# A decoder layer's gate rows by DMA, a put-off weight remainder and two exchanged PSUM pools

## The chip, the cores and the metric

The kernel runs on one core of one Trainium2 chip. The metric is device time in microseconds (us) of one execution, taken as the median of several runs.

## The reference

One inference step of a two-layer decoder: 256 prompt tokens and 64 sample tokens (8 sequences of 8) share the weights. Layer 0 mixes tokens with a gated MLP, layer 1 with an mLSTM, and each is followed by a gated MLP with a short convolution. The change lies in the mLSTM, of 8 heads with keys of 128 and values of 256. What matters of it, cut:

```
m_t = max(inter, max(D))             # D = b_t - b_s + i_s, inter = b + m
w_intra = exp(D - m_t);  w_inter = exp(inter - m_t)
sc  = (q k^T) * w_intra
num = w_inter * (q C) + sc v
den = w_inter * (q n) + sum(sc)
h   = num / max(|den|, exp(-m_t))
C_new = decay * C + (k * g)^T v      # decay = exp(bL + m - m_new)
hn  = (h - mean(h)) * rsqrt(var(h) + eps) * gain
y   = (sigmoid(o) * hn) @ w_out
```

The prompt starts from an empty state; each of the 8 sample sequences has a state C of its own, which is read and written back.

## The kernel before

**Layout.** Activations lie with features on the partitions and the 320 tokens along the free dimension. Each fp32 weight block of 128 columns (a tile `raw`, 512 KB) comes by DMA on SP's queue and is split into two parts, `wh` by a cast on ScalarE and the remainder `wl = raw - wh` by VectorE (`prefetch`, lines 120 to 157). A product is three matmuls per 128 rows: wh with xh, wh with xl, wl with xh. In this layer `low_last` is set, so that a block issues its 16 matmuls with wh first and the 8 with wl last (`chunk`, line 173). There are four buffers of `raw` and three each of `wh` and `wl`; taking a block starts the load of the fourth block behind it and the split of the next one (`take`, line 165).

**PSUM.** There are two pools of banks: `psm` with three, mostly for the blocks (`pm`), and `psa` with five, for everything else. A tile takes the bank that came free first, so that in psm the tile after next but one waits for the readers of the present one, in psa the fifth after it.

**Order.** TensorE's order is the program's, pinned by `mm` and `tr`. The other engines' order comes from a planner that runs instructions by program order among those that it holds ready, by its own costs; `tc.issue_after(x)` sets instructions behind x on x's engine, and `pin` keeps one in the program's order. Each engine, and each DMA queue, then works strictly in its order.

**Gates (line 661).** From the gate weights the kernel makes, for all heads at once, rows of eight partitions, `Xf`, 392 long: 320 running maxima, 64 factors for the sample tokens and 8 decays of the states. They are kept in two parts in `X`. `sel` (128 x 8 x 128) holds for each head a matrix that picks its row and spreads it over all partitions.

**Heads (lines 1057 to 1115).** Iteration h goes through six blocks: q (`qk_epi(h, 0)`), k, two of v (`v_epi`), two of the output gate (`o_epi`, line 993). Between them lies the end of head h-1: its states' part (`inter`), `numer`, `stats`, `state_prompt`, and its four pairs of state updates, `state_sample(h-1, 0..3)`, each with two matmuls into `pcs` (one bank in psa, one in psm up to head 5), two updates of `C` on VectorE and a store. `scores(h)` (line 789) spreads the head's row over the partitions with a matmul into `pMb` (`sel[:, h]` against `X`), makes the scores `psc`, the weights `w` from pMb by three Exp on ScalarE with masks by GpSimd, copies the decays to `dec`, and scales the sample's queries to `qw`. Behind the second gate block come `finish(h-1)` (transposes of `hn` into two tiles `phn`, then `y_b`, `yhb`, `ylb`, line 1000), `state_sample(h-1, 3)`, `k_nat(h)` (three transposes into `pk`, line 855), `v_nat(h)` (six into two tiles `pv`) and `inter(h, 0)` (into `num`). For h = 4, 5 and 6 blocks of the output projection (`early`) are put in.

**stats (line 931)** makes mean, variance and denominator of `num`; GpSimd raises to the power -1/2 (`sl`, line 953), VectorE makes the bias `nb` (line 957), and ScalarE writes the normalised `hn`. In the last head a function `between`, with the first gate block's end and a split of weights, stands ahead of `nb`.

**Tail (lines 1118 to 1149).** For the last head two banks of psm hold begun output blocks (`begin`), so that the two gate blocks share the third.

The lines that say most:

```
1101                if h and not last:
1102                    o_epi(h, 1, blk())
1103                if h and not last:
1104                    finish(h - 1)
1105                    state_sample(h - 1, 3)
1106                k_nat(h)
1107                v_nat(h)
```

Of the kernel before, what the change touches and what calls it, by code (L numbers as in the profile page):

```python
# [37 lines left out]
class Net:  # L38
# [26 lines left out]
    def weights(self):  # L65

        I = self.I
        q = []

        def add(w, b, *groups, k0=0):  # L70
            for kn in groups:
                q.append((w, b, k0, kn))
                k0 += kn


        add(I["a_wv"], 0, 4)
        add(I["a_wv"], 4, 4)
        add(I["a_wv"], 0, 4, k0=4)
        for b in range(1, 4):
            add(I["a_wv"], b, 4, 4)  # L80
        add(I["a_wv"], 4, 4, k0=4)
        for b in range(5, 16):
            add(I["a_wv"], b, 8)
        for b in range(16):
            add(I["a_win"], b, 8)
        for b in range(KD):
            add(I["a_wo"], b, 8, 8)

        def ffn(l):
            for b in range(2 * KF):  # L90
                add(I["f_up"][l], b, 8)
            for b in range(KD):
                add(I["f_dn"][l], b, 8, 7, 7)

        ffn(0)
        add(I["b_wg"], 0, 8)
        for h in range(NH):
            for r in range(6):
                r = (0, 2, 1, 3, 4, 5)[r] if h == 0 else r
                if (h, r) == (NH - 1, 4):  # L100
                    for k0, n in ((8, 4), (12, 2)):
                        for b in (0, 1):
                            add(I["b_wo"], b, n, k0=k0)
                add(I["b_win"], 6 * h + r, 8)
                for b in self.EARLY_OUT.get((h, r), ()):
                    add(I["b_wo"], b, 8)
        add(I["b_wo"], 2, 6, k0=8)
        for b in (0, 1, 2):
            add(I["b_wo"], b, 2, k0=14)
        for b in range(3, KD):  # L110
            add(I["b_wo"], b, 8, k0=8)
        ffn(1)
        self.wq = q
        self.loaded, self.halved, self.used = [], [], 0

    AHEAD, SPLIT_AHEAD = 4, 1
    low_last = False
# [2 lines left out]
    def prefetch(self, n, m):  # L120

        nc = self.nc
        while len(self.loaded) < min(n, len(self.wq)):
            w, b, k0, kn = self.wq[len(self.loaded)]
            raw = self.wraw.tile([P, 8, P], F32, tag="raw", name="raw")
            for j, z in ((0, 2), (2, 4)) if len(self.loaded) < 2 else ((0, kn),):
                self.hold(nc.sync.dma_start(raw[:, j:z, :], w[b, :, k0 + j:k0 + z, :]))
            self.loaded.append(raw)
        while len(self.halved) < min(m, len(self.wq)):
            i = len(self.halved)  # L130
            raw, kn = self.loaded[i], self.wq[i][3]
            self.loaded[i] = None
            wh = self.wsp.tile([P, 8, P], F32R, tag="wh", name="wh")
            wl = self.wsp.tile([P, 8, P], F32R, tag="wl", name="wl")
            if self.wq[i][0] is self.I["b_wg"]:

                nc.scalar.copy(wh[:, :, 64:], raw[:, :, 64:])
                nc.scalar.copy(wl[:, :, :64], raw[:, :, :64])
                nc.vector.tensor_tensor(wl[:, :, 64:], raw[:, :, 64:], wh[:, :, 64:].bitcast(F32), op=SUB)
                self.halved.append((None, wl))  # L140
                continue
            if i < 2:

                a, z = slice(0, 2), slice(2, 4)
                if not i:
                    self.hold(nc.vector.tensor_copy(wh[:, a, :], raw[:, a, :]))
                    self.x_parts(0)
                for c in (a, z)[not i:]:
                    self.last_split = self.hold(nc.scalar.copy(wh[:, c, :], raw[:, c, :]))
                for c in (a, z):  # L150
                    self.last_low = self.hold(nc.vector.tensor_tensor(wl[:, c, :], raw[:, c, :], wh[:, c, :].bitcast(F32), op=SUB))
                self.halved.append((wh, wl))
                continue
            self.last_split = self.hold(nc.scalar.copy(wh[:, :kn, :], raw[:, :kn, :]))  # L154
            self.last_low = nc.vector.tensor_tensor(wl[:, :kn, :], raw[:, :kn, :], wh[:, :kn, :].bitcast(F32), op=SUB)  # L155
            self.hold(self.last_low)
            self.halved.append((wh, wl))

    @contextmanager
    def behind_split(self):  # L160
# [21 lines left out]
                if sweep:  # L182
                    self.mm(ps[:, :T], wl[:, k, :], xh, False, last and k == kn - 1)

    def block(self, kt, rhs):

        ps = self.psm.tile([P, 512], F32, tag="pm", name="pm")
        done = 0
        while done < kt:
            kn = self.wq[self.used][3]  # L190
            self.chunk(ps, lambda k: rhs(done + k), done == 0, done + kn == kt)
            done += kn
        return ps
# [441 lines left out]
    def layer_b(self):  # L635
# [5 lines left out]
        with ExitStack() as ctx:  # L641
# [3 lines left out]
            gnh = lp.tile([P, 16], F32, name="gnh")  # L645
            colsT = lp.tile([P, 3, 96], F32, name="cols")
            X = lp.tile([P, 392], F32R, name="X")
            sel = lp.tile([P, NH, P], F32R, name="sel")
            mk = lp.tile([P, NB], F32, name="mk")
            mo = lp.tile([8, 9], F32, name="mo")  # L650
            pads = []
# [9 lines left out]
            def gates(rp):  # L661

                bif = rp.tile([40, 1 + NB], F32, name="bif")
                rst = rp.tile([40, 2, T], F32, name="rst")
                selr = rp.tile([P, NH, P], F32, name="selr")
                RS = rp.tile([P, 384], F32, name="RS")
                nc.sync.dma_start(bif, I["b_if"])
                nc.sync.dma_start(rst, I["seg"])
# [54 lines left out]
                nc.vector.tensor_tensor(seg(wi[:, :64]), m0.unsqueeze(2).to_broadcast([8, NB, NS]), seg(M[:, TP:]), op=SUB)  # L723
                nc.vector.tensor_tensor(wi[:, 64:72], m0, ML, op=SUB)
                nc.scalar.activation(Xf[:, T:392], wi, AF.Exp)
                nc.vector.tensor_copy(X[0:8], Xf)
                nc.vector.tensor_tensor(X[32:40], Xf, X[0:8].bitcast(F32), op=SUB)
                nc.vector.tensor_scalar(gnh, self.vecs[:, V_GN:V_GN + 16], 0.5, None, op0=MULT)
# [54 lines left out]
            def v_epi(h, j, ps):  # L783
# [2 lines left out]
                nc.scalar.copy(vT[:, T:384], ps[:, TP:T])  # L786
                S[h].setdefault("vT", []).append(vT)

            def scores(h):
                s = S[h]  # L790
                q, qh, ql = s["q"]
                k, kh, kl = s["k"]
                pb = self.psa.tile([P, 512], F32, tag="pa", name="pMb")
                sc = self.psa.tile([P, 512], F32, tag="pa", name="psc")
                if h:
                    mm(pb[:, :392], sel[:, h, :], X, True, True)
                mm3(sc[:, :TP], kh, kl, qh, ql, True, True)
                mm(sc[:, TP:384], k[:, P:TP], q[:, P:TP], True, True)
                mm(sc[:, 384:448], k[:, TP:384], q[:, TP:T], True, True)
                if not h:  # L800

                    mm(pb[:, :392], sel[:, h, :], X, True, True)
                w = hp.tile([P, 448], F32, tag="w", name="w", bufs=1)
                for (n, o, c0, c1, t) in ((P, 0, 0, TP, 0), (P, TP, P, TP, 1), (64, 384, TP, T, 2)):
                    nc.scalar.activation(w[:n, o:o + c1 - c0], pb[:n, c0:c1], AF.Exp, scale=-1.0, bias=colsT[:n, t, h:h + 1])
                for o in (0, TP):
# [4 lines left out]
                                        channel_multiplier=1)  # L811
                nc.gpsimd.affine_select(w3, w3, pattern=[[NS, NB], [1, NS]], compare_op=ALU.is_ge, fill=0.0, base=0,
                                        channel_multiplier=-1)
                dec = hp.tile([P, NB], F32, tag="dec", name="dec", bufs=2)
                nc.vector.tensor_copy(dec, pb[:, 384:392])
                qw = hp.tile([P, 64], F32, tag="qw", name="qw", bufs=1)
                nc.vector.scalar_tensor_tensor(qw, q[:, TP:T], 0.5, pb[:, T:384], op0=MULT, op1=MULT)
                Qd = Qz.rearrange("p (b e) -> p b e", e=136)
# [36 lines left out]
            def k_nat(h):  # L855
                s = S[h]
                ks = s["k"][0]
                pk = self.psa.tile([P, 512], F32, tag="pa", name="pk")
                for t in range(3):
                    self.tr(pk[:, t * P:(t + 1) * P], ks[:, t * P:(t + 1) * P], self.ident)  # L860
                kgh = hp.tile([P, 2, P], F32R, tag="kgh", name="kgh", bufs=1)
# [69 lines left out]
            def stats(h, between=None):  # L931
# [17 lines left out]
                t1 = hp.tile([P, 3], F32, tag="t1", name="t1", bufs=1)  # L949
                nc.vector.scalar_tensor_tensor(t1, rd, EPS, rd, op0=MULT, op1=MULT)  # L950
                self.t_made = nc.vector.scalar_tensor_tensor(t1, t1, 1e-36, mv[:, :, 1], op0=MAX, op1=ADD)
                sl = hp.tile([P, 3], F32, tag="sl", name="sl", bufs=1)
                nc.gpsimd.tensor_tensor(sl, t1, self.mhalf.to_broadcast([P, 3]), op=ALU.pow)
                if between:
                    between()
                nb = hp.tile([P, 3], F32, tag="nb", name="nb", bufs=1)
                made = nc.vector.scalar_tensor_tensor(nb, mv[:, :, 0], -1.0, sl, op0=MULT, op1=MULT)
                if between:
                    self.pin(made)
                for t in range(3):  # L960
                    n = P if t < 2 else 64
                    if h == NH - 1 and t:
# [37 lines left out]
            def finish(h):  # L1000
# [3 lines left out]
                for e in range(2):  # L1004
# [1 line left out]
                    for t in range(3):  # L1006
                        self.tr(pt[:, t * P:(t + 1) * P], hn[:, t, e * P:(e + 1) * P], self.ident)
                    y = self.tp.tile([P, T], F32, tag="yf", name="y_b", bufs=2)
                    nc.vector.scalar_tensor_tensor(y, s["o"][e], 1.0, pt[:, :T], op0=ADD, op1=MULT)
                    g = gnh[:, 2 * h + e:2 * h + e + 1]  # L1010
                    nc.scalar.activation(yh[:, e, :], y, AF.Copy, scale=g)
                    nc.vector.scalar_tensor_tensor(yl[:, e, :], y, g, yh[:, e, :].bitcast(F32), op0=MULT, op1=SUB)
# [43 lines left out]

            for h in range(NH):
                if h:
                    qk_epi(h, 0, blk())
                    early(h, 0)  # L1060
                    if h == 1:
# [35 lines left out]
                if h:  # L1097
                    state_in(h)
                    for i in (0, 1):
                        state_split(h, i)  # L1100
                if h and not last:
                    o_epi(h, 1, blk())
                if h and not last:
                    finish(h - 1)
                    state_sample(h - 1, 3)
                k_nat(h)
# [26 lines left out]
            v_first(h)  # L1133
            state_prompt(h)
            k_mask(h)
            o_epi(h, 1, blk())
            finish(h)
            state_sample(h, 0)
            begin(2)
            state_sample(h, 1)  # L1140
            for m in range(KD):
                ps = part.get(m)
# [61 lines left out]
def _lay_out(i):  # L1204
# [55 lines left out]
    seg[:, 0, starts] = 0.0  # L1260
    seg[:, 1, starts] = -1e30
    a["seg"] = seg
    sel = np.zeros((P, NH, P), f)
    for h in range(NH):
        sel[h, h] = 1.0
        sel[32 + h, h] = 1.0
    a["sel"] = sel

    b, q = np.arange(NB), s // 32
# [30 lines left out]
```

## Time and profile before

| | |
|---|---|
| median of 3 runs | 956.14 us (955.89 to 956.53) |
| the profiled execution's own time | 956.05 us |
| its span, first to last instruction | 954.3 us |
| TensorE / VectorE / ScalarE / GpSimd busy | 99% / 73% / 56% / 12% |
| mean granted TensorE clock | 0.999 |
| mean DMA rate | 163 GB/s |

The span is what the trace covers; about 1.7 us of the execution lie outside it. A row of a timeline has the start in us from the span's start, the length in us, engine, line, operation, what is written and from what, and a count; in square brackets stands how long the engine sat idle just before, and which instruction ended that. Matmuls overlap, so their cost is the distance between starts and not their length.

### The profile page before, as it was taken

How to read it: one execution, taken by the hardware profiler on the slowest of the kernel's cores; microseconds unless marked ns; L12 is line 12 of the kernel's file. 1: busy time of each engine (PE TensorE's matmuls, PEld its weight loads, DVE VectorE, ACT ScalarE, POOL GpSimd, SP SyncE). 2: the span in 40 equal slices, each digit the busy share in tenths (PEclk: the TensorE clock that was granted, in tenths of full speed). 3: DMA queues.
4: the chain of work that ended last, by engine and by line, in shares of the span. 5: the costliest groups of instructions: out<-in, count | busy, mean ns of one | idle time of the engine just before them, and what ended most of it. 6: DMA issues, size and time to landing. Idle time of an engine off the chain costs nothing.

```text
span 954.3 us, 17131 instructions
## 1 busy us (share of the span) xinstructions
PE 947.3 (99%) x6427; PEld 933.8 (98%) x6427; DVE 697.3 (73%) x1331; ACT 531.9 (56%) x978; POOL 115.8 (12%) x291
## 2 busy tenths in 40 slices
PE   9999999999999999999999999999999999999997
PEld 8889999999999999999999999999999999999997
DVE  6766976577777754559999998788897777775443
ACT  7557543454555443458777876666766445544342
POOL 2200000010000000014333322102102000000000
PEclk9999999999999999999999999999999999999999
DMA  8643346444444465565465655553474444445441
GB/s 270 210 153 133 133 137 198 160 146 147 149 156 155 139 183 147 149 216 175 128 212 175 206 178 196 185 183 118 132 247 148 149 145 154 156 144 155 143 141 56
DMA packets 54214, 155.19 MB, mean 163 GB/s; under 512 B 7372, under 2 KB 11980, under 8 KB 54132
## 3 DMA queue, kind: packets, MB, share of 16 engines
q1 hardware_dynamic: 54132, 154.10, 50.5%
q8 instruction: 51, 0.84, 0.4%
q14 instruction: 31, 0.25, 0.1%
HBM read 142.10 MB, written 11.97 MB: 161 GB/s over the span
## 4 chain that ended last, share of the span: by engine, by line
PE 94%; DVE 3%; ACT 1%; POOL 1%; DMA 0%; issue 0%; SPq 0%; POOLq 0%
PE pm L54 81%; PE pv_a L54 6%; PE num L54 2%; PE pmix L54 1%; PE pcs L54 1%; PE psc L54 1%; PE phn L57 0%; PE pCp L54 0%; DMA raw<-in_a_wv 0%; PE pv L57 0%; DVE wl L155 0%; PE pc L54 0%; DVE bcv L767 0%; PE pg L54 0%; PE pk L57 0%
## 5 line engine op out<-in xcount | busy, mean ns | idle before, releaser
L154 ACT CAST wh<-raw 128x1024 fp32r<-128x1024 f32 (+3 forms) x256 | 257.0, 1004 | 294.1 <-PE pm L54 161.7
L155 DVE TENSOR_TENSOR wl<-raw,wh 128x1024 fp32r<-128x1024 f32 (+3 forms) x256 | 299.0, 1169 | 118.9 <-ACT wh L154 115.0
L54 PE MATMUL pm<-xh,wh 128*128 128x320 f32 x1216 | 372.3, 311 | 0.1
L54 PE MATMUL pm<-xl,wh 128*128 128x320 f32 x1216 | 370.3, 309 | 0.0
L54 PE MATMUL pm<-xh,wl 128*128 128x320 f32 x1216 | 321.2, 309 | 0.0
L54 PEld LDWEIGHTS pm<-xh,wh 128*128 128x128 f32 x1216 | 228.4, 188 | 0.4 <-DVE o_b L995 0.3
L54 PEld LDWEIGHTS pm<-xl,wh 128*128 128x128 f32 x1216 | 228.4, 188 | 0.2
L54 PEld LDWEIGHTS pm<-xh,wl 128*128 128x128 f32 x1216 | 214.5, 188 | 0.0
L54 PE MATMUL pm<-yh_f,wh 128*128 128x320 f32 x352 | 108.8, 309 | 0.0
L54 PE MATMUL pm<-yl_f,wh 128*128 128x320 f32 x352 | 108.8, 309 | 0.0
L54 PE MATMUL pm<-yh_f,wl 128*128 128x320 f32 x352 | 108.8, 309 | 0.0
L54 PEld LDWEIGHTS pm<-yh_f,wh 128*128 128x128 f32 x352 | 66.1, 188 | 0.0
L54 PEld LDWEIGHTS pm<-yl_f,wh 128*128 128x128 f32 x352 | 66.1, 188 | 0.0
L54 PEld LDWEIGHTS pm<-yh_f,wl 128*128 128x128 f32 x352 | 66.1, 188 | 0.0
L531 DVE SCALAR_TENSOR_TENSOR fcv<-fpad,vecs,fcv 128x336 f32<-128x336 f32 x88 | 49.6, 565 | 2.1 <-ACT fcv L529 0.7
L54 PE MATMUL pm<-yh_a,wh 128*128 128x320 f32 x128 | 39.6, 310 | 0.0
L54 PE MATMUL pm<-yh_a,wl 128*128 128x320 f32 x128 | 39.5, 309 | 0.0
L54 PE MATMUL pm<-yl_a,wh 128*128 128x320 f32 x128 | 39.5, 309 | 0.0
L533 ACT ACTIVATE fgl<-fcv 128x256 f32<-128x256 f32 x44 | 18.2, 414 | 37.8 <-DVE fcv L531 37.8
L54 PE MATMUL pm<-yhb,wh 128*128 128x320 f32 x128 | 38.1, 311 | 0.0
L54 PE MATMUL pm<-ylb,wh 128*128 128x320 f32 x128 | 37.8, 309 | 0.0
L303 DVE TENSOR_TENSOR xT<-pm,xT 128x320 f32<-128x320 f32 x39 | 19.1, 489 | 25.1 <-PE pm L54 24.9
(286 smaller groups left out, 1371.7 us busy)
## 6 DMA issues: line engine op xcount, KB each, us to landing
raw<-in_f_up SPq DMA_DIRECT2D x88, 512.0 KB, 3.3
raw<-in_b_win SPq DMA_DIRECT2D x48, 512.0 KB, 4.0
raw<-in_f_dn SPq DMA_DIRECT2D x32, 448.0 KB, 3.3
C<-in_C SPq DMA_DIRECT2D x32, 258.0 KB, 3.7
out_Cs<-C SPq DMA_DIRECT2D x32, 258.0 KB, 2.5
raw<-in_a_win SPq DMA_DIRECT2D x16, 512.0 KB, 3.3
raw<-in_a_wo SPq DMA_DIRECT2D x16, 512.0 KB, 4.3
raw<-in_f_dn SPq DMA_DIRECT2D x16, 512.0 KB, 3.5
```

The lines of the kernel that those rows point to most:

```text
L54: self.pin(self.nc.tensor.matmul(out, lhsT, rhs, start=start, stop=stop, skip_group_check=skip))
L154: self.last_split = self.hold(nc.scalar.copy(wh[:, :kn, :], raw[:, :kn, :]))
L155: self.last_low = nc.vector.tensor_tensor(wl[:, :kn, :], raw[:, :kn, :], wh[:, :kn, :].bitcast(F32), op=SUB)
L303: self.nc.vector.tensor_tensor(x, ps[:, :T], x, op=ADD)
L531: nc.vector.scalar_tensor_tensor(cv, pd[:, i:i + NC], self.vec(w + i * KF), cv, op0=MULT, op1=ADD)
L533: nc.scalar.activation(gl[:, :TP], cv[:, :TP], AF.Gelu_apprx_tanh)
```

## The change

It has seven edits, all but the small `sel` in or for the heads' loop:

- `Xf` is stored to a DRAM tensor `rows`, and each head from 1 on loads its row from there into all partitions, a tile `Mb` of two buffers. Head 0 keeps the matmul. `sel` shrinks to head 0's matrix.
- For these heads `dec` is a part of `Mb`, and isn't copied.
- In heads 1 to 6 the remainder `wl` of the block behind the second gate block is put off until the first `y_b` of `finish`.
- `pk` takes its bank in psm, but for the last head.
- `nb` is made by GpSimd from the negated mean, ahead of `between`.
- The last head's second gate block takes its bank in psa.
- Behind `begin(2)` one more block is split ahead.

The small name for it is "with two such transposes": `finish` transposes into two tiles as before; nothing in the diff touches that.

```diff
@@ prefetch
             self.last_split = self.hold(nc.scalar.copy(wh[:, :kn, :], raw[:, :kn, :]))
-            self.last_low = nc.vector.tensor_tensor(wl[:, :kn, :], raw[:, :kn, :], wh[:, :kn, :].bitcast(F32), op=SUB)
-            self.hold(self.last_low)
             self.halved.append((wh, wl))
+            self.late.append((wl[:, :kn, :], raw[:, :kn, :], wh[:, :kn, :]))
+            if not self.put_off:
+                self.low_parts()
+
+    def low_parts(self):
+
+        for wl, raw, wh in self.late:
+            self.last_low = self.hold(self.nc.vector.tensor_tensor(wl, raw, wh.bitcast(F32), op=SUB))
+        self.late = []
@@ gates
-            sel = lp.tile([P, NH, P], F32R, name="sel")
+            sel = lp.tile([P, P], F32R, name="sel")
...
                 nc.scalar.activation(Xf[:, T:392], wi, AF.Exp)
+
+                nc.sync.dma_start(I["rows"], Xf)
@@ scores
+            def rows_in(h):
+                mb = hp.tile([P, 392], F32, tag="Mb", name="Mb", bufs=2)
+                nc.sync.dma_start(mb, I["rows"][h:h + 1, :].to_broadcast([P, 392]))
+                S[h]["rows"] = mb
...
-                pb = self.psa.tile([P, 512], F32, tag="pa", name="pMb")
+                pb = s["rows"] if h else self.psa.tile([P, 512], F32, tag="pa", name="pMb")
...
-                if h:
-                    mm(pb[:, :392], sel[:, h, :], X, True, True)
...
-                    mm(pb[:, :392], sel[:, h, :], X, True, True)
+                    mm(pb[:, :392], sel, X, True, True)
...
-                dec = hp.tile([P, NB], F32, tag="dec", name="dec", bufs=2)
-                nc.vector.tensor_copy(dec, pb[:, 384:392])
+                dec = pb[:, 384:392]
+                if not h:
+                    dec = hp.tile([P, NB], F32, name="dec")
+                    nc.vector.tensor_copy(dec, pb[:, 384:392])
@@ k_nat
-                pk = self.psa.tile([P, 512], F32, tag="pa", name="pk")
+                pool, tag = (self.psm, "pm") if h < NH - 1 else (self.psa, "pa")
+                pk = pool.tile([P, 512], F32, tag=tag, name="pk")
@@ stats
+                nm = hp.tile([P, 3], F32, tag="nm", name="nm", bufs=1)
+                nc.vector.tensor_scalar(nm, mv[:, :, 0], -1.0, None, op0=MULT)
                 sl = hp.tile([P, 3], F32, tag="sl", name="sl", bufs=1)
                 nc.gpsimd.tensor_tensor(sl, t1, self.mhalf.to_broadcast([P, 3]), op=ALU.pow)
+                nb = hp.tile([P, 3], F32, tag="nb", name="nb", bufs=1)
+                nc.gpsimd.tensor_tensor(nb, nm, sl, op=MULT)
                 if between:
                     between()
-                nb = hp.tile([P, 3], F32, tag="nb", name="nb", bufs=1)
-                made = nc.vector.scalar_tensor_tensor(nb, mv[:, :, 0], -1.0, sl, op0=MULT, op1=MULT)
-                if between:
-                    self.pin(made)
@@ finish
-                    nc.vector.scalar_tensor_tensor(y, s["o"][e], 1.0, pt[:, :T], op0=ADD, op1=MULT)
+                    made = nc.vector.scalar_tensor_tensor(y, s["o"][e], 1.0, pt[:, :T], op0=ADD, op1=MULT)
+                    if self.put_off:
+                        self.put_off = False
+                        with tc.issue_after(made.ins):
+                            self.low_parts()
@@ the heads' loop
                 if h:
+                    rows_in(h)
                     qk_epi(h, 0, blk())
...
                 if h and not last:
+                    self.put_off = True
                     o_epi(h, 1, blk())
-                if h and not last:
                     finish(h - 1)
                     state_sample(h - 1, 3)
@@ the tail
-            o_epi(h, 1, blk())
+            o_epi(h, 1, self.block(KD, self.x_rhs, self.psa.tile([P, 512], F32, tag="pa", name="pm")))
             finish(h)
             state_sample(h, 0)
             begin(2)
+            self.prefetch(0, self.used + 2)
```

`block` gets an argument for a PSUM tile of the caller's.

More of the change, by code (lines that the diff above doesn't have):

```diff
@@ L114, in weights @@
         self.loaded, self.halved, self.used = [], [], 0
+        self.late, self.put_off = [], False
     AHEAD, SPLIT_AHEAD = 4, 1
@@ L183, in chunk, with block @@
                     self.mm(ps[:, :T], wl[:, k, :], xh, False, last and k == kn - 1)
-    def block(self, kt, rhs):
-        ps = self.psm.tile([P, 512], F32, tag="pm", name="pm")
+    def block(self, kt, rhs, ps=None):
+        if ps is None:
+            ps = self.psm.tile([P, 512], F32, tag="pm", name="pm")
         done = 0
@@ L664, in gates @@
                 rst = rp.tile([40, 2, T], F32, name="rst")
-                selr = rp.tile([P, NH, P], F32, name="selr")
+                selr = rp.tile([P, P], F32, name="selr")
                 RS = rp.tile([P, 384], F32, name="RS")
@@ L1262, in _lay_out @@
     a["seg"] = seg
[L1263 to L1266, printed above, removed]
+    sel = np.zeros((P, P), f)
+    sel[[0, 32]] = 1.0
     a["sel"] = sel
@@ L1282 @@
     I = {k: nc.dram_tensor("in_" + k, v.shape, F32, kind="ExternalInput").ap() for k, v in arrays.items()}
+    I["rows"] = nc.dram_tensor("rows", (NH, 392), F32).ap()
     O = {k: nc.dram_tensor("out_" + k, s, F32, kind="ExternalOutput").ap() for k, s in _OUTS.items()}
```

## The prediction

> **What bounds the kernel now.** I read the page first, for the busy shares.
>
> ```profile
> span 954.3 us, 17131 instructions
> PE 947.3 (99%) x6427; PEld 933.8 (98%) x6427; DVE 697.3 (73%) x1331; ACT 531.9 (56%) x978; POOL 115.8 (12%) x291
> ```
>
> TensorE (PE) is busy for 99% of the span. So time can be won in two ways only: fewer matmuls, or fewer of PE's waits. All edits but the small selector lie in the mLSTM layer's loop over heads, about 446 to 694 us. Next I read the view of stretches there: one between heads 1 and 2, one head of six weight blocks, one of eight.
>
> ```profile
> 479.70:489.30 9.60, 9.60 (x71) 9.60 (x70) 9.42 (x20) 8.34 (x17) 4.37 (x6) 1.00 0.62 195
> 508.20:536.70 28.50, 28.50 (x209) 28.49 (x209) 26.82 (x66) 21.91 (x51) 10.00 (x13) 1.00 0.59 181
> 565.20:604.35 39.15, 39.15 (x282) 39.14 (x281) 32.19 (x72) 25.17 (x54) 6.91 (x13) 1.00 0.57 184
> ```
>
> After the length come PE, weight loads, VectorE (DVE), ScalarE and GpSimd (POOL) busy, then the clock, 1.00. DVE is second: 98% behind head 1, 94% in head 3, 82% in head 5. Third, the waits of PE's weight loads in the whole layer, of which two can be touched:
>
> ```profile
> PEld pv L57 <- DVE y_b L1009: 0.8, 1, 0.8
> PEld pm L54 <- DVE o_b L995: 0.3, 1, 0.3
> ```
>
> **The selector matmul.** Seven of the eight pMb matmuls go (heads 1 to 7). What one costs is the distance of two starts on PE's timeline, since matmuls overlap.
>
> ```profile
> 525.91 0.34 PE L54 MATMUL pMb<-X,sel 128*128 128x392 f32 x1
> 526.10 0.28 PE L54 MATMUL psc<-qh,kh 128*128 128x256 f32 x1
> ```
>
> 526.10 − 525.91 = 0.19 us, by times rounded to 0.01; I take 0.18. PE never waits there, so all of it is on the path: 7 × 0.18 = **1.26 us** less. The Trainium skill, "TensorE: Matmul & The Clock Gate", section "Wait — 56ns, not 53.3ns?", gives columns ÷ 2.4 GHz plus about 2.5 ns for a warm start-to-start: an estimate of 166 ns for 392 columns, and of 1.16 us for seven. The trace's 0.19 us is longer, and the sum keeps the trace.
>
> **Its replacement** is one 12.5 KB store and seven loads of 128 × 1568 B = 196 KB on SP's queue. Nearest rows:
>
> ```profile
> C<-in_C SPq DMA_DIRECT2D x32, 258.0 KB, 3.7
> gB<-in_a_ln_g SPq DMA_DIRECT2D x4, 128.0 KB, 5.0
> ```
>
> The second is also a row repeated over partitions. So a load lands 3.7 to 5.0 us after issue; I take 5.0. It is issued at a head's start and wanted in its scores, four blocks of 3.5 us later: 14 us of cover. I cost it at 0. Each load waits on SP for the reader of the buffer two heads back, the last state update, and weight loads queue behind it; the store of that same update waits there now, so the place of the wait isn't new. The small selector shortens one cast on ScalarE in head 0's gates, of which PE waits for nothing; and ScalarE and DVE read the row from SBUF instead of PSUM, off PE's path. Both 0.
>
> **Head 1's wait.** PE's timeline in head 1, and the same two steps in head 5:
>
> ```profile
> 476.93 0.49 PE L57 MATMUL pk<-ident,qs 128*128 128x128 f32 x3
> 477.26 0.60 PE L57 MATMUL pv<-ident,vTb 128*128 128x128 f32 x4
> 478.44 0.44 PE L57 MATMUL pv<-ident,vTb 128*128 128x128 f32 x2 [0.58 <-DVE y_b L1009]
> 478.93 0.36 PE L54 MATMUL num<-Ch,Qz 128*128 128x258 f32 x1
> ...
> 603.04 0.82 PE L57 MATMUL pv<-ident,vTb 128*128 128x128 f32 x6
> 603.62 0.36 PE L54 MATMUL num<-Ch,Qz 128*128 128x258 f32 x1
> ```
>
> From pv to num head 5 takes 0.58 us, head 1 takes 1.67: the wait costs 1.09. The second pv tile is the fifth psa bank after the first phn, so it waits for the y_b that reads phn. DVE at that time:
>
> ```profile
> 473.45 1.21 DVE L155 TENSOR_TENSOR wl<-raw,wh 128x1024 fp32r<-128x1024 f32 x1
> 474.58 0.55 DVE L311 TENSOR_TENSOR Pl<-Pf,Ph 128x384 fp32r<-128x384 f32 x1
> ...
> 476.37 1.22 DVE L155 TENSOR_TENSOR wl<-raw,wh 128x1024 fp32r<-128x1024 f32 x1
> ...
> 477.91 0.87 DVE L1009 SCALAR_TENSOR_TENSOR y_b<-th_o,phn 128x320 f32<-128x320 f32 x2
> ```
>
> ```profile
> 473.31 0.51 ACT L311 CAST Ph<-Pf 128x384 fp32r<-128x384 f32 x1 [0.30 <-DVE Pf L824]
> ```
>
> There are 256 such wl, as many as weight chunks, so counting in queue order tells whose each is: the one at 473.45 is head 2's first block, which the change puts behind the first y_b; the one at 476.37 belongs to the block after and stays. Without the former, DVE moves up until Pl meets its input at 473.82: by 0.7 us. The first y_b then ends near 478.39 − 0.7 = 477.7. With pk in psm, one bank fewer is asked of psa, so the next to wait is num, which PE reaches at 478.93 − 1.09 − 0.18 = 477.66. About 0.1 is left: **1.0 us** gained. The bounds are 0 (DVE only carries the lateness on) and 1.09.
>
> **What putting off costs.** In head 3:
>
> ```profile
> 527.95 1.22 DVE L155 TENSOR_TENSOR wl<-raw,wh 128x1024 fp32r<-128x1024 f32 x1
> ...
> 534.45 0.49 DVE L995 TENSOR_TENSOR o_b<-pm,rb 128x320 f32<-128x320 f32 x1 [0.53 <-PE pm L54]
> 534.86 0.88 DVE L1009 SCALAR_TENSOR_TENSOR y_b<-th_o,phn 128x320 f32<-128x320 f32 x2
> ```
>
> ```profile
> 538.88 1.34 PE L54 MATMUL pm<-xh,wl 128*128 128x320 f32 x8
> ```
>
> The wl of 527.95 would run behind the first y_b, from about 535.3 to 536.5, and PE reads it at 538.88: 2.4 us to spare. The raw buffer comes free some 7 us later, inside a lead of four blocks. Queued behind it on DVE are the second y_b, state updates, k and v remainders, all about 1.13 us later (start to start, 473.45 to 474.58). The tightest that I found is k's remainder for the next scores:
>
> ```profile
> 523.17 0.29 DVE L311 TENSOR_TENSOR khl<-qs,kh 128x128 fp32r<-128x128 f32 x1
> ```
>
> It ends at 523.46 and psc starts at 526.10: 2.6 us, of which 1.5 remain. So 0; the bounds are 0 and 1.13 in each of six heads.
>
> **The last gate block.** In the tail, PE waits for a bank (the o_b row among the waits above):
>
> ```profile
> 695.66 1.22 DVE L155 TENSOR_TENSOR wl<-raw,wh 128x1024 fp32r<-128x1024 f32 x1
> ```
>
> ```profile
> 683.89 0.28 PE L54 MATMUL pCp<-vh,kgl 128*128 128x258 f32 x1
> 684.22 0.42 PE L54 MATMUL pm<-xh,wh 128*128 128x320 f32 x1
> 684.47 0.31 PE L54 MATMUL pm<-xl,wh 128*128 128x320 f32 x1
> ...
> 697.10 1.34 PE L54 MATMUL pm<-yhb,wl 128*128 128x320 f32 x8
> ```
>
> The block's first steps take 0.33 + 0.25 us where 0.12 and 0.15 are usual: 0.31 lost. The psa bank is free by then. But at 697.10 PE comes only 0.22 us behind the wl that ends at 696.88, so I count **0.2 us** (bounds 0 and 0.31). The earlier split after begin(2) removes no wait that the timeline shows and adds no instruction: 0.
>
> **pk in psm, head 0.** The next block then takes the bank of head 0's second gate block:
>
> ```profile
> 448.74 0.48 DVE L995 TENSOR_TENSOR o_b<-pm,rb 128x320 f32<-128x320 f32 x1
> ...
> 457.11 0.69 DVE L902 TENSOR_TENSOR Cl<-C,Ch 128x516 fp32r<-128x516 f32 x1
> ```
>
> ```profile
> 448.87 0.39 PE L54 MATMUL pm<-xh,wh 128*128 128x320 f32 x1
> ...
> 457.44 0.28 PE L54 MATMUL num<-Ch,Qz 128*128 128x258 f32 x1
> 457.85 0.39 PE L54 MATMUL num<-Cl,Qz 128*128 128x258 f32 x1
> ```
>
> It could start at about 449.28 instead of 448.87: 0.4 us. But at 457.85 PE waits 0.3 for Cl anyway, and DVE, not PE, is late there; that absorbs most. **+0.05 us** (bounds 0 and 0.41).
>
> **Bias on POOL.** The nearest rows:
>
> ```profile
> L762 POOL COPY bns<-bpad x16: 185/468/1244, 430.3 to 658.5; 128x3 f32<-128x3 f32 x16
> 682.98 1.49 POOL L953 TENSOR_TENSOR sl<-t,mhalf 128x3 f32<-128x3 f32 x1 [12.62 <-DVE t L951]
> ```
>
> 0.19 to 1.49 us on POOL for 0.16 on DVE; I take 0.47. ScalarE's hn waits for it, with casts of weights for later blocks queued behind, and two blocks of PE lie before hn is transposed. The copy of dec (0.16 us on DVE) is off PE's path. Both 0.
>
> **Sum.** −1.26 − 1.0 − 0.2 + 0.05 = −2.4. The profiled execution took 956.05 us, of which 1.7 lie outside the span; the median is 956.14. Forecast: **953.7 us**, its own range 953.1 to 954.3. A measurement of this kernel tells about 0.2% (1.9 us) from no change, so the forecast is just beyond that.
>
> **Rivals.**
> *The wait only moves* (21%). DVE had 0.18 us idle between heads 1 and 2; with PE a microsecond earlier, another DVE output is late. For it: 98%. Against it: the margins of 1.5 us and more. Then −1.4: 954.7.
> *The put-off remainder is late work* (17%, the slower side). DVE waits 0.5 us for o_b now, and would wait 1.2 more with nothing to do, then lag by 1.13. It decides from where a head has less idle DVE time than that to catch up: head 3 has 28.50 − 26.82 = 1.68, head 5 has 7. If six heads lose it: +6.8 − 2.4, so 960.4; if three (6%): 957.1, no change.
> *A transfer is late* (6%): a blocked SP delays one weight load by its landing, 4 us by C's row: 957.6, no change.
> *DVE and POOL stretch each other* (3%).
>
> ```profile
> 452.91 1.16 DVE L311 TENSOR_TENSOR Pl<-Pf,Ph 128x384 fp32r<-128x384 f32 x1
> ```
>
> Pl takes 0.55 in head 1 and 1.16 here, beside a POOL product. Six such, uncovered, give 6 × 0.6 − 2.4: 957.3. The Trainium skill, "SBUF — State Buffer", section "Who interferes with whom", says that a DVE instruction with two SBUF inputs and a POOL one that reads SBUF lock each other out; by that rule qw, now with two SBUF inputs, joins them, and the row agrees.
> *All waits vanish* (5%): −1.26 − 1.09 − 0.31 − 0.3 = −3.0: 953.1.
>
> **How the numbers follow.** Forecast 42%. Faster by over 0.2% (below 954.2): 42 + 5, 0.47; within: 21 + 6 + 6 + 3, 0.36; slower (above 958.0): 0.17. The range goes from 952.9, the case without waits less what the runs of before scatter below their median (0.25), to 957.7, the late transfer; it leaves out only the last 17%.
>
> **What would show it.** pMb once in the after profile; no PE wait on y_b or o_b in the layer; the wl behind y_b landing over 1 us ahead of its matmuls; DVE's wait for o_b near 1.7 us. PE waits on khl, wl or Cl in heads 2 to 7 would make it wrong.

## The result, and the profile after

| kernel | median | range | runs | ratio to before (95% interval) |
|---|---|---|---|---|
| before | 956.03 us | 955.89 to 956.53 | 4 | |
| changed | 967.14 us | 966.37 to 967.79 | 4 | 1.0115 (1.0097 to 1.0132) |

The change costs 11.1 us. The forecast was 953.7, the range ended at 957.7. The profiled execution, the longest of the four, took 967.79 us, with a span of 965.6, 11.3 more than before. The busy line of the profile, and the waits of TensorE's (PE's) weight loads in the layer (us in total, times, longest), as they were shown of before:

```profile
PE 949.0 (98%) x6420; PEld 934.1 (97%) x6420; DVE 698.9 (72%) x1324; ACT 530.6 (55%) x978; POOL 118.5 (12%) x299
```

```profile
PEld pm L54 <- DVE wl L164: 8.3, 6, 1.8
PEld pcs L54 <- ACT vTb L797: 2.8, 1, 2.8
PEld num L54 <- DVE Cl L919: 1.1, 1, 1.1
PEld pm L54 <- DVE o_b L1012: 0.4, 1, 0.4
```

PE has seven matmuls fewer, as foreseen, and VectorE (DVE) and ScalarE (ACT) have about the work of before: 698.9 us against 697.3, 530.6 against 531.9. What is new are waits. Two kinds make nearly the whole loss: six times the remainder `wl` of a weight block is late, once the copy `vTb` of v.

**The late remainder.** VectorE around the second gate block of head 2, before and after:

```profile
504.24 1.22 DVE L155 TENSOR_TENSOR wl<-raw,wh 128x1024 fp32r<-128x1024 f32 x1
505.92 0.49 DVE L995 TENSOR_TENSOR o_b<-pm,rb 128x320 f32<-128x320 f32 x1 [0.47 <-PE pm L54]
```

```profile
509.39 0.49 DVE L1012 TENSOR_TENSOR o_b<-pm,rb 128x320 f32<-128x320 f32 x1
509.80 0.48 DVE L1026 SCALAR_TENSOR_TENSOR y_b<-th_o,phn 128x320 f32<-128x320 f32 x1
510.20 1.22 DVE L164 TENSOR_TENSOR wl<-raw,wh 128x1024 fp32r<-128x1024 f32 x1
...
516.93 0.48 DVE L862 SCALAR_TENSOR_TENSOR vl<-pv,rc,vh 128x256 fp32r<-128x256 f32 x1
517.32 1.22 DVE L164 TENSOR_TENSOR wl<-raw,wh 128x1024 fp32r<-128x1024 f32 x1
```

And PE there, after:

```profile
513.83 1.34 PE L54 MATMUL pm<-xh,wl 128*128 128x320 f32 x8
...
517.67 0.31 PE L54 MATMUL pm<-xl,wh 128*128 128x320 f32 x1
518.59 1.46 PE L54 MATMUL pm<-xh,wl 128*128 128x320 f32 x8 [0.61 <-DVE wl L164]
```

The remainder that the change puts off is the one at 510.20. It runs right behind the first y_b and ends at 511.42; PE reads it at 513.83, 2.4 us later: this part came as forecast. But the remainder of the block after it, which before ran 1.7 us ahead of o_b, now stands 7.9 us behind o_b, at 517.32, behind the second y_b and most of the k and v remainders. It ends at 518.54, and PE starts with it at 518.59: 0.92 us after the matmul before, where 0.15 is usual. Which block each remainder belongs to comes from counting in queue order, as in the prediction. By the same count the cast `wh` that the late remainder needs starts at 504.86 on ScalarE, so its input was there in time, and the order alone made it late. Counted by starts in this way, the six waits cost 0.8, 0.8, 1.3 and three times 1.6 us beyond the usual, and with 0.1 us each for the step behind them **8.4 us**.

**The late copy.** Head 1's statistics on GpSimd (POOL), VectorE and ScalarE, and PE, all after:

```profile
468.15 3.25 POOL L972 TENSOR_TENSOR sl<-t,mhalf 128x3 f32<-128x3 f32 x1 [2.35 <-DVE t L968]
471.48 0.20 POOL L974 TENSOR_TENSOR nb<-nm,sl 128x3 f32<-128x3 f32 x1
```

```profile
468.12 1.21 DVE L164 TENSOR_TENSOR wl<-raw,wh 128x1024 fp32r<-128x1024 f32 x1
469.26 0.21 DVE L836 TENSOR_TENSOR Qz<-qw,Qz 128x64 fp32r<-128x64 f32 x1
469.39 1.29 DVE L919 TENSOR_TENSOR Cl<-C,Ch 128x516 fp32r<-128x516 f32 x2
470.61 0.86 DVE L1007 SCALAR_TENSOR_TENSOR C<-C,dec,pcs 128x258 f32<-128x258 f32 x2
```

```profile
471.71 1.02 ACT L982 ACTIVATE hn<-num,nb,sl 128x256 f32<-128x256 f32 x2 [3.23 <-POOL nb L974]
...
473.12 1.03 ACT L155 CAST wh<-raw 128x1024 fp32r<-128x1024 f32 x1
474.05 0.42 ACT L796 COPY vTb<-pm 128x320 f32<-128x320 f32 x1
```

```profile
471.82 0.28 PE L54 MATMUL pcs<-vb,kgz 128*128 128x258 f32 x1
474.63 0.39 PE L54 MATMUL pcs<-vb,kgz 128*128 128x258 f32 x1 [2.53 <-ACT vTb L797]
```

Before, the power took 0.86 us, and VectorE stood idle at its end:

```profile
468.98 0.16 DVE L957 SCALAR_TENSOR_TENSOR nb<-mv,sl 128x3 f32<-128x3 f32 x1 [0.57 <-POOL sl L953]
```

After, VectorE has nothing to wait for and runs `wl`, Qz and two Cl, all with two operands in SBUF. The power, of three elements a partition, takes 3.25 us. The bias itself is cheap (0.20). ScalarE stands 3.23 us at the first hn, and behind the hn's and a cast the copy of v comes at 474.05, where it came at 470.58 before. Of these 3.5 us the later hn's are 2.5, and 0.9 is the cast, which before stood behind the copy. PE waits 2.7 us (2.81 from start to start, 0.12 is usual).

Then PE is slow for a while. The stretches (length, PE busy, granted clock, DMA share and GB/s):

```profile
471.90:474.60 2.70, 0.20 (x2) 1.00 0.78 243
474.86:475.73 0.87, 0.87 (x7) 1.00 0.01 5
475.73:479.15 3.42, 3.42 (x15) 0.50 0.48 159
```

From 475.73 to 479.15 the granted clock is 0.50, and matmuls start every 0.27 us instead of every 0.15. That and the step behind the wait (0.1) cost another 1.6 us. Head 1's loss is **4.3 us**. The last head's wait for Cl (the third line of waits) costs 1.2, and head 0's block that waits for o_b 0.4. Against these 14.3 us stand 1.3 for the matmuls, 1.1 for head 1's old wait, 0.3 in the tail and 0.4 for a wait of head 0 on Cl: 3.1 less. That makes 11.2 of the 11.3 us between the spans.

### The profile page after: what moved, and what is told of

The parts are those of the page before. It is cut to its first block, busy times and chain, and to the rows that moved or that the text cites. A ratio compares the mean times of both kernels' runs of the same rounds, so it can differ in the third digit from the quotient of the medians.

```text
span 965.6 us, 17111 instructions
## 1 busy us (share of the span) xinstructions
PE 949.0 (98%) x6420; PEld 934.1 (97%) x6420; DVE 698.9 (72%) x1324; ACT 530.6 (55%) x978; POOL 118.5 (12%) x299
## 4 chain that ended last, share of the span: by engine, by line
PE 84%; DVE 9%; ACT 3%; issue 1%; DMA 1%; POOL 1%; SPq 0%; ACTq 0%; DVEq 0%
PE pm L54 73%; PE pv_a L54 6%; DVE wl L164 2%; PE num L54 2%; DVE Cl L919 1%; PE pmix L54 1%; DVE C L1007 1%; POOL sl L972 1%; ACT wh L155 1%; DMA Mb<-rows 1%; ACT hn L982 0%; DVE ylb L1033 0%; DVE bcv L778 0%; DVE o_b L1012 0%; PE pcs L54 0%
```

## The experiments

Each ratio is to the kernel before on the same chip (956.2 to 956.3 us).

| kernel | median, us | range, us | ratio (95% interval) |
|---|---|---|---|
| next_first | 960.15 | 959.33 to 962.37 | 1.0048 (1.0035 to 1.0062) |
| no_putoff | 960.28 | 959.47 to 961.13 | 1.0042 (1.0030 to 1.0055) |
| nb_dve | 963.38 | 963.11 to 963.55 | 1.0074 (1.0061 to 1.0086) |
| next_first_nb_dve | 958.32 | 955.90 to 959.37 | 1.0017 (1.0008 to 1.0026) |
| no_putoff_nb_dve | 955.66 | 955.24 to 956.64 | 0.9994 (0.9985 to 1.0003) |
| before_putoff | 963.96 | 963.80 to 964.54 | 1.0082 (1.0069 to 1.0094) |
| before_nb_pool | 961.46 | 960.99 to 961.91 | 1.0055 (1.0042 to 1.0067) |
| before_rows | 956.80 | 956.24 to 958.34 | 1.0005 (0.9996 to 1.0014) |
| dve_held | 963.88 | 963.22 to 964.13 | 1.0077 (1.0063 to 1.0091) |
| before_pk_psm | 955.85 | 955.25 to 956.26 | 0.9994 (0.9986 to 1.0003) |
| before_last_psa | 956.06 | 955.45 to 956.52 | 0.9996 (0.9987 to 1.0005) |
| best1 | 954.99 | 953.95 to 957.31 | 0.9987 (0.9978 to 0.9996) |

**1. next_first: the next block's split, and so its remainder, written ahead of the put-off remainder.**

```diff
                     self.put_off = True
                     o_epi(h, 1, blk())
+                    late, self.late, self.put_off = self.late, [], False
+                    self.prefetch(0, self.used + 2)
+                    self.late, self.put_off = late, True
                     finish(h - 1)
```

> The changed kernel, but the low parts of the block behind the put-off one are written into the program ahead of the put-off ones; the putting off stays. Theory A (the putting off itself is free, and its price of about 8.4 us is that it pushed the next block's low parts behind y_b and the k and v remainders, where six matmuls wait 0.79, 0.78, 1.26, 1.64, 1.65 and 1.63 us for them and then start about 0.1 us later still): all six waits go, 967.1 - 8.4 = 958.7 us (958 to 960), with the 2.7-us wait of head 1 for ACT's copy still there. Rival B (VectorE has no room for a subtract of 1.2 us behind y_b, whichever block it belongs to): the waits stay or move to the put-off parts, 965 us or more.

Measured: 960.15, 7.0 us less than the changed kernel. No wait for a remainder is left in the layer. VectorE in the same place of the same head:

```profile
506.43 1.21 DVE L164 TENSOR_TENSOR wl<-raw,wh 128x1024 fp32r<-128x1024 f32 x1
507.64 0.49 DVE L1012 TENSOR_TENSOR o_b<-pm,rb 128x320 f32<-128x320 f32 x1
...
508.44 1.22 DVE L164 TENSOR_TENSOR wl<-raw,wh 128x1024 fp32r<-128x1024 f32 x1
```

Both subtracts fit, the next block's ahead of o_b and the put-off one behind y_b. So VectorE has room, and rival B falls: it was the order. The median is 0.15 us beyond the end of theory A's range. Of the 1.4 us to its 958.7 most is a new wait of 1.2 us for kh in one head, which experiment 4 shows larger.

**2. no_putoff: the changed kernel without the putting off.**

```diff
                 if h and not last:
-                    self.put_off = True
                     o_epi(h, 1, blk())
```

> The changed kernel without the putting off: every subtract stands where the kernel before has it; rows by DMA, bias by GpSimd, the pool of the last gate block and of the k transposes stay. Theory A: the six waits for low parts go, and the wait ahead of the v transposes of head 1 may come back (1.1 us): 958.7 to 959.8 us. Rival B: the same here, so this run bounds what the putting off costs in all. Rival C (the k transposes' new pool or the rows' DMA delays VectorE, and the low parts with it): waits for low parts stay, 963 us or more.

Measured: 960.28. Theory A again, 0.5 us above its upper end; rival C's late remainders aren't there. The rest is theory D's, in more heads: the power takes 3.25 us in each of heads 1 to 4, and the copy of v is late four times:

```profile
PEld pcs L54 <- ACT vTb L797: 4.3, 4, 2.8
```

**3. nb_dve: the changed kernel with the bias made by VectorE** (`nm` and GpSimd's product out, the old `scalar_tensor_tensor` back behind `between`).

> The changed kernel with the bias made by VectorE as before, the rest changed. Theory D (with the bias on GpSimd VectorE no longer waits for the power of -0.5, runs its own long instructions beside it, and the power takes 3.25 us in head 1 instead of 0.86; ScalarE stands before the first normalisation and its copy of v comes 2.7 us late, and TensorE then runs 13 matmuls at half speed): the power is back near 0.86 us in head 1, the wait goes, 967.1 - 4.4 = 962.7 us (962 to 964). Rival E (ScalarE is late in head 1 for the rows' or the block order's sake, the bias plays no part): the wait stays, 966 to 967.5 us.

Measured: 963.38, 3.8 us less than the changed kernel; PE no longer waits for vTb. Theory D, but the power is not back at 0.86:

```profile
468.10 1.91 POOL L970 TENSOR_TENSOR sl<-t,mhalf 128x3 f32<-128x3 f32 x1 [2.27 <-DVE t L968]
```

```profile
468.07 1.21 DVE L164 TENSOR_TENSOR wl<-raw,wh 128x1024 fp32r<-128x1024 f32 x1
470.04 0.16 DVE L974 SCALAR_TENSOR_TENSOR nb<-mv,sl 128x3 f32<-128x3 f32 x1 [0.76 <-POOL sl L970]
```

One subtract stands ahead of nb here. It ends at 469.28, the power at 470.01, 0.73 us later. In the changed kernel the row of wl, Qz and two Cl ends at 470.68 and the power at 471.40: 0.72 us later. In both the power ends a fixed time after the last of an unbroken row of VectorE instructions with two SBUF operands.

**4. next_first_nb_dve: 1 and 3 in one.**

> Both repairs in one: next block's low parts ahead of the put-off ones, and the bias by VectorE. Theories A and D add up: 967.1 - 8.4 - 4.4 = 954.3 us (953.5 to 955.5), faster than the kernel before by 1 to 2 us, since the row matmuls (1.26 us) and the wait ahead of head 1's v transposes (1.0) are gone. If the two losses overlap or another is hidden behind them: 957 us or more.

Measured: 958.32, between 955.9 and 959.4 from run to run. Not the 954.3 of the sum. No remainder and no copy of v is late, but twice the scores wait for kh. VectorE and PE:

```profile
524.52 1.21 DVE L164 TENSOR_TENSOR wl<-raw,wh 128x1024 fp32r<-128x1024 f32 x1
525.66 0.41 DVE L782 SCALAR_TENSOR_TENSOR qs<-bth,bcv 128x256 f32<-128x256 f32 x1
```

```profile
524.93 0.40 PE L54 MATMUL pcs<-vh,kgz 128*128 128x258 f32 x2
526.45 0.39 PE L54 MATMUL psc<-qh,kh 128*128 128x256 f32 x1 [1.11 <-ACT kh L320]
```

A subtract now stands ahead of qs, from which kh is cast, and scores start 1.5 us after the matmuls before them. So putting off isn't free with the order mended either: other instructions come late a head later. How the moved subtract brings that about was not followed through the queue. Against experiment 5 it costs 2.7 us by the medians.

**5. no_putoff_nb_dve: 2 and 3 in one.**

> The changed kernel without the putting off and with the bias by VectorE: rows by DMA, the k transposes' pool, the pool of the last gate block and its early split are left. Theory A with D: both losses are gone, and the row matmuls are saved: 956.2 - 1.3 = 954.9 us, down to 953.8 if head 1's wait is gone too (953.8 to 956). If the k transposes' pool or the rows' DMA have a price of their own that the two losses hid: 957 us or more.

Measured: 955.66, no difference that can be told from before. The two losses make 11.5 us together: 967.14 − 955.66. Alone they gave 6.9 and 3.8; each is worth 0.9 more with the other gone.

**6. before_putoff: the putting off alone, in the kernel before.**

> The kernel before with the putting off alone (all heads from 1 to 6). Theory A: the next block's low parts fall behind y_b and the k and v remainders here too, six waits on low parts, 8.4 us less the 1.0 us of head 1's wait: 963.6 us (961.5 to 965). Rival F (the k transposes in the other pool, and not the putting off, let the planner draw the k and v remainders ahead of the low parts): at most 957 us.

Measured: 963.96, theory A's number, but not by its waits: no remainder is awaited. VectorE and PE in head 2:

```profile
506.67 0.48 DVE L1017 SCALAR_TENSOR_TENSOR y_b<-th_o,phn 128x320 f32<-128x320 f32 x1
507.06 1.22 DVE L164 TENSOR_TENSOR wl<-raw,wh 128x1024 fp32r<-128x1024 f32 x1
...
508.66 0.48 DVE L1017 SCALAR_TENSOR_TENSOR y_b<-th_o,phn 128x320 f32<-128x320 f32 x1
...
513.47 1.22 DVE L164 TENSOR_TENSOR wl<-raw,wh 128x1024 fp32r<-128x1024 f32 x1
```

```profile
507.22 0.82 PE L57 MATMUL pv<-ident,vTb 128*128 128x128 f32 x6
509.29 0.36 PE L54 MATMUL num<-Ch,Qz 128*128 128x258 f32 x1 [1.25 <-DVE y_b L1017]
```

Here pk takes a psa bank, so num needs the bank of the second phn and waits for the second y_b, behind the put-off subtract: 2.07 us from pv to num instead of 0.58, in each of six heads. That comes near the prediction's rival "the put-off remainder is late work", at 1.5 us a head where the rival had 1.13. Theory A's reordering is here too: the following remainder, at 513.47, stands 7.2 us behind o_b and behind six k and v remainders, and so it does in all six heads. So the putting off alone makes that order, and not pk's pool; rival F falls by its mechanism as well as by its 957. PE, already late for y_b, reads that remainder only at 516.17. In the changed kernel, with pk in psm, there is no such wait for y_b, and PE waits for the remainder instead. That theory A's sum was met is chance.

**7. before_nb_pool: the bias by GpSimd alone, in the kernel before.**

> The kernel before with the bias by GpSimd alone. Theory D: the power in head 1 takes about 3.2 us instead of 0.86, ScalarE's copy of v is late and TensorE waits and then runs slowly: 956.2 + 4.4 = 960.6 us (959 to 961.5). Rival E (the long power needs the other order that the putting off gives VectorE): the power stays below 2 us and the time within 0.5 us of 956.2.

Measured: 961.46, within theory D's range, but mostly in another place. In head 1 the power takes 0.86 us; it starts 0.31 us ahead of a subtract. There the product that makes the bias is the long one, 1.24 us beside that subtract and a Cl, and PE waits 0.8 us for vTb. In heads 2 to 4 the power takes 2.98.

```profile
497.03 2.98 POOL L955 TENSOR_TENSOR sl<-t,mhalf 128x3 f32<-128x3 f32 x1 [2.34 <-DVE t L951]
```

```profile
PEld pv L57 <- DVE y_b L1009: 4.2, 4, 1.1
```

ScalarE normalises late, y_b is late, and the wait that only head 1 had before now stands in heads 1 to 4.

**8. before_rows: the rows by DMA alone.**

> The kernel before with the rows by DMA alone, seven selector matmuls of 0.18 us fewer. As in the prediction: 956.2 - 1.26 = 954.9 us (954.5 to 955.3). Rival: the row's landing of 4 to 5.5 us, which made ScalarE wait up to 2.2 us in the runs above, reaches TensorE or moves VectorE's order: 956 us or more.

Measured: 956.80, no gain; the rival's end. The loads' own landing is as forecast, and ScalarE waits for them three times:

```profile
Mb<-rows SPq DMA_DIRECT2D x7, 196.0 KB, 4.3
```

But PE's new waits aren't on the rows. Two of them in the last head:

```profile
676.75 0.28 PE L54 MATMUL num<-Ch,Qz 128*128 128x258 f32 x1
677.51 0.39 PE L54 MATMUL num<-Cl,Qz 128*128 128x258 f32 x1 [0.48 <-DVE Cl L909]
...
683.29 0.28 PE L54 MATMUL pCp<-vh,kgl 128*128 128x258 f32 x1
684.14 0.41 PE L54 MATMUL pm<-xh,wh 128*128 128x320 f32 x1 [0.57 <-DVE o_b L1002]
```

```profile
674.09 1.23 DVE L155 TENSOR_TENSOR wl<-raw,wh 128x1024 fp32r<-128x1024 f32 x1
```

Without dec's copy and with qw free early, the planner sets this subtract ahead of the second kgs, of vl and of Cl; before it stood behind Cl. Cl costs 0.64 and o_b 0.52 more than before, and a pcs in head 1 another 0.43 for its bank: 1.6 us for the 1.3 saved.

**9. dve_held: the changed kernel, and VectorE waits for GpSimd's bias.**

```diff
                 nc.gpsimd.tensor_tensor(nb, nm, sl, op=MULT)
                 if between:
                     between()
+                held = nc.vector.tensor_scalar(nm, nb, 1.0, None, op0=MULT)
+                if between:
+                    self.pin(held)
```

> The changed kernel, bias still by GpSimd, but VectorE is made to wait for it: a copy of the bias (3 elements a partition, nobody reads it) stands in VectorE's order where the bias was made before. Theory D (GpSimd's power is long because VectorE runs long instructions with two operands from SBUF beside it, and not because GpSimd has one instruction more): the power of head 1 falls from 3.25 us to about 1.9, as where VectorE makes the bias, and the time to that kernel's 963.4 us (963 to 964). Rival G (the bias on GpSimd, and ScalarE's wait for it, are what costs): no change, 966 to 967.5 us.

Measured: 963.88. GpSimd has the same two instructions as in the changed kernel, and one wait of VectorE more makes the kernel 3.3 us faster:

```profile
468.49 1.90 POOL L972 TENSOR_TENSOR sl<-t,mhalf 128x3 f32<-128x3 f32 x1 [2.34 <-DVE t L968]
```

So rival G falls for nearly all of the loss: it isn't where the bias is made, but what VectorE does meanwhile. The 0.5 us above experiment 3 may be what is left of it: PE still waits 0.8 us for vTb, since here, as in the changed kernel, a cast of 1.03 us stands between the hn's and the copy, and in experiment 3 it stands ahead of the hn's.

**10. before_pk_psm: pk's pool alone.**

> The kernel before with the k transposes of heads 0 to 6 in the other pool alone. Prediction's step: nothing but 0.05 us. Theory H (this shift alone frees the bank that head 1's v transposes wait for, so that the putting off had nothing left to gain): the waits of 0.96 us in head 1 go and 956.2 - 1.0 = 955.2 us (955 to 955.6). If not: 956 to 956.4 us.

Measured: 955.85; the interval holds both answers, the span is the 954.3 of before. In the trace head 1's wait of 0.96 us is 0.61 (num now waits, for th_o), head 0's on Cl (0.29) is gone, and head 0's block waits 0.33 for its bank. Theory H holds for a third of the wait.

**11. before_last_psa: the last gate block's pool and the early split alone.**

> The kernel before with the last gate block in the other pool and its early split alone. Prediction's step: -0.2 us (0 to 0.31), 956.0 us. Rival: nothing, 956.2, or the early split costs, 956.5 or more.

Measured: 956.06, not to be told from before. In the trace the wait for o_b in the tail is gone, as in the prediction's step.

**12. best1: no_putoff_nb_dve with two orders written out.**

```diff
-                    o_epi(h, 0, blk())
+                    with tc.issue_after(self.nb_made.ins):
+                        ps = blk()
+                    o_epi(h, 0, ps)
...
-            begin(0)
-            begin(1)
+            with tc.issue_after(self.cl_made.ins):
+                begin(0)
+                begin(1)
```

(`nb_made` and `cl_made` are the bias and the last Cl.)

> The changed kernel without the putting off and with the bias by VectorE, and two orders written out: the low parts of the gate block are issued behind the bias, so that the power runs alone, and in the last head the low parts of the block that follows stand behind the last state split. If the shorter power and the state split take away the waits left in head 1 (0.43 and 0.43 us) and in the last head (0.64): 955.7 - 1.5 = 954.2 us (953.8 to 955). If the waits only move: 955.4 to 956.

Measured: 954.99, 1.35 us below before's 956.34 and below all the others, by little: the interval ends at 0.9996. The last head's wait for Cl is gone. The power is 1.37 us, since a Cl (468.69 to 469.37) has taken the subtract's place beside it, and it ends at 470.09, again 0.72 us behind:

```profile
468.72 1.37 POOL L970 TENSOR_TENSOR sl<-t,mhalf 128x3 f32<-128x3 f32 x1 [2.28 <-DVE t L968]
```

Head 1's two waits of 0.43 us stayed, so that part of the expectation fell.

## Why the prediction was wrong

- **Selector matmuls, −1.26: right as a term.** pMb is written once. But it isn't a gain by itself (experiment 8): about as much is lost to an order that shifts.
- **The rows' load, 0: nearly right.** Landing was 4.5 us for my 5.0. The cover wasn't the 14 us that I gave it, since ScalarE waited for a row in two heads (1.4 us); no wait of PE was traced to it.
- **Head 1's wait, −1.0: right in size.** From pv to num it now takes 0.57 us, as in head 5. What does it is more than the putting off: pk's new bank takes a third (experiment 10), and where the rows come by DMA, too, 0.43 is left without putting off (experiment 5).
- **"The one at 476.37 belongs to the block after and stays": this step failed**, and with it "What putting off costs", 0. This is the sign that I had named against myself, PE waits on wl in heads 2 to 7. I moved one instruction in the queue of before and left all others where they stood. The put-off one did as forecast, with 2.4 us to spare. But the order is made anew by the planner for the changed program, and it set the following remainder among the k and v remainders, 9.6 us later against o_b than before. My bound of 1.13 us a head had the wrong cause, and in four heads it was too small (1.3 and three times 1.6). Experiment 1, where only the order in the program is mended, and 2, without the putting off, have none of the six waits; experiment 6 has the same order from the putting off alone.
- **Last gate block, −0.2: right** (0.3 gone in the trace). **pk in head 0, +0.05: right**, 0.33 lost and 0.29 won, not counting the steps behind (0.1 each).
- **"Bias on POOL ... Both 0": this step failed.** I priced the moved instruction (0.47; it took 0.20), and took the two blocks ahead of hn's transposes for its cover. But DVE's old nb was also a wait, and behind that wait VectorE started nothing while GpSimd worked. Without it the power of head 1 takes 3.25 us; in heads 2 to 6 it takes 1.76, where a C update or khl follows the subtract. And I named the weight casts behind hn on ScalarE, but not the copy of v, which PE wants first. 3.8 us in experiment 3, 4.6 between experiments 2 and 5.
- **The rivals.** "The put-off remainder is late work" gave 960.4 (953.7 + 6.8 makes 960.5) and was the right side; a wait like it is shown in experiment 6 and not in the changed kernel. "DVE and POOL stretch each other", at 3%, is what happened to the power, though I priced it for Pl only and for qw, not for an instruction that loses its quiet. Two losses at once were in no case.

Not settled: why the planner holds the following remainder back once the one ahead is put off. That the order in the program decides it is shown (experiment 1), and that the putting off alone brings it about (experiment 6); the planner's inner reason was not looked for. Nor was it tried to keep kh from being late with the putting off (experiment 4).

## What to carry to other kernels

An instruction that waits is doing something if another engine works undisturbed meanwhile: before taking a wait away, look at what will run in its place, and beside what. Where a planner orders the queues, moving one instruction is a new order for all that follow it; forecast from the whole list of what may pass it, and write out the order of those that have a deadline. A gain of one microsecond on TensorE can be lost to a shifted order elsewhere: in experiment 8, 1.6 us for the 1.3 saved.

## What the runs showed of the hardware

- GpSimd's power of three elements a partition took 0.85 to 0.86 us beside a VectorE that was idle or at a C update, 1.37 beside one Cl, 1.76 or 1.90 beside one wl (begun 0.16 or 0.03 us ahead of the power), 3.25 beside wl, Qz and two Cl. In these rows it ended 0.71 to 0.73 us after the last of them, and two C updates, with one operand in PSUM, ran beside that last part without stretching it. One case doesn't fit: in heads 5 and 6 of experiment 9 a khl of 0.28 us, also with two operands in SBUF, follows the subtract at once, and the power still ends 0.71 us after the subtract. Why khl doesn't hold it is open. Begun 0.31 us ahead of a subtract the power wasn't stretched, but the product behind it was (experiment 7: 1.24 us for 0.20). The Trainium skill, "SBUF — State Buffer", section "Who interferes with whom", says that a VectorE instruction with two SBUF inputs contends with a GpSimd one that reads SBUF, and that the order of issue decides who is blocked; but for khl these rows agree.
- After 2.7 us without work in the changed kernel PE went on at full clock for 1.1 us (474.63 to 475.73) and then at 0.50 for 3.4 us. In experiment 2 the same wait (2.81 us from start to start) was followed by 0.50 almost at once, again for 3.4 us. In experiment 1 (2.80 us) the clock stayed at 1.00. Experiment 2's slow stretch, then experiment 1's wait and what follows it:

```profile
474.72:478.13 3.41, 3.41 (x13) 0.50 0.46 142
```

```profile
472.60:475.20 2.60, 0.17 (x2) 1.00 0.73 277
476.30:479.10 2.80, 2.80 (x21) 1.00 0.55 186
```

The Trainium skill, "TensorE: Matmul & The Clock Gate", section "What's actually happening", speaks of an idle window of about 3.4 us that runs freely; here less was enough, in two of three traces. So such a wait costs itself alone, or itself and half as much again; what decides between the two these runs don't show.
